# Contrast adjustment: every store on ScalarE's DMA queue, the last tile in two column halves, and sums shared with VectorE in all tiles

## The chip, the cores and the metric

The kernel runs on one core of one Trainium2 chip. The metric is device time in microseconds for one execution. Before the change it is 240.2 us, the median of 3 runs (240.01 to 240.23). One more execution was profiled; all views below are of that one.

## The reference

```
mean = np.mean(x, axis=(2, 3), keepdims=True)
return np.clip(mean + factor * (x - mean), 0, 1).astype(np.float32)
```

`x` is float32 of shape 16 x 3 x 512 x 512, 50.33 MB, and the output has the same size; `factor` is 1.5. Each of the 48 images of 512 x 512 has its own mean, and a pixel can be finished only when its whole image has been summed.

## The kernel before, in words

The input is read as 6 tiles of 128 partitions x 16384 floats (64 KB in a partition, 8.39 MB in a tile). A tile holds 8 images of 16 partitions each. Three tiles fit in SBUF: `ring` has `BUFS = 3` slots, and tile t lies in slot t mod 3. So the load of tile t+3 waits until every store of tile t has landed. Everything is done in place in the slot.

The steps of one tile are:

- **Load** (`load`, L78): a DMA issued by SyncE (SP). Tile 0 comes in three pieces (2048, 6144 and 8192 columns), the others whole.
- **Sum** (`add`, `sum_up`, L87 and L90): ScalarE (ACT) copies a range of columns onto itself with `accum_out`, which leaves each partition's sum. VectorE (DVE) sums another range with a `tensor_reduce`. For tile 0 each half is shared (VectorE takes `SUM` = 4352 columns and ScalarE 3840 of each half). For tiles 1 and 2 VectorE takes 4352 and ScalarE 12032 columns. For tiles 3, 4 and 5 ScalarE sums all 16384 columns.
- **Shift** (L104): TensorE multiplies the partial sums by `blockw`, a block matrix with `(1 - factor) / n_pix` in blocks of 16 x 16. This adds the 16 partitions of each image and leaves the shift of every partition in PSUM. There is one matmul in the code for each partial sum, accumulated.
- **Clip** (L107 and L110): two VectorE `tensor_scalar` instructions over a range of columns, x * factor + shift, then max 0 and min 1. Both lines together are called the clip pair below.
- **Store** (`store`, L81): a DMA issued by the queue that is handed in. The stores of tiles 0, 1 and 2 and the first quarter of tile 3 (4096 columns) are issued by ScalarE; the other three quarters of tile 3, and tiles 4 and 5 whole, by SP.

The order on each engine is the order in the code, since the schedule is written out by hand. Each engine takes its instructions strictly in order, DMA issues included: an issue that waits for a semaphore holds up whatever stands behind it on its engine. SP issues all 8 loads first (the loads of tiles 3, 4 and 5 each with their waits), and then the three last stores. ScalarE alternates sums and stores until the first quarter of tile 3, and has only sums after that.

In the text, "store 3a" is the first quarter of tile 3 and "store 3b" its other three quarters. A "row" of a DMA is what it moves for one partition: 128 rows in each DMA, 64 KB long for a whole tile, and shorter for a range of columns.

Of the kernel before, what the change touches and what calls it, by code (L numbers as in the profile page):

```python
# [1 line left out]

# [4 lines left out]


P = 128  # L10
ROW = 16384
HALF = ROW // 2
BUFS = 3
SHORT = 2048
SUM = 4352
QUARTER = ROW // 4


@with_exitstack
def kernel(  # L20
    ctx: ExitStack,
    tc: tile.TileContext,
    x: bass.AP,
    factor: float,
    out: bass.AP,
):

    nc = tc.nc  # L30
    f32 = mybir.dt.float32
    Alu = mybir.AluOpType
    Act = mybir.ActivationFunctionType

    B, C, H, W = x.shape
    n_img, n_pix = B * C, H * W
    ppi = n_pix // ROW
    per_tile = P // ppi
    n_tiles = n_img // per_tile
    assert ppi * ROW == n_pix and per_tile * n_tiles == n_img  # L40

    factor = float(factor)
    wconst = (1.0 - factor) / float(n_pix)

    x_f = x.rearrange("b c h w -> (b c h w)")
    out_f = out.rearrange("b c h w -> (b c h w)")

    def dram(ap, t, c0=0, c1=ROW):
        return bass.AP(tensor=ap.tensor, offset=t * P * ROW + c0, ap=[[ROW, P], [1, c1 - c0]])

    consts = ctx.enter_context(tc.tile_pool(name="consts", bufs=1))
    xpool = ctx.enter_context(tc.tile_pool(name="xpool", bufs=1))
    small = ctx.enter_context(tc.tile_pool(name="small", bufs=1))
    psum = ctx.enter_context(tc.tile_pool(name="psum", bufs=1, space=bass.MemoryType.PSUM))


    sums = small.tile([P, 4 * n_tiles], f32, name="sums")
    bias = psum.tile([P, n_tiles], f32, name="bias")

    blockw = consts.tile([P, P], f32, name="blockw")  # L60
    blocks = blockw.rearrange("p (a b) -> p a b", b=ppi)
    nc.gpsimd.memset(blockw, wconst)  # L62
    for base, step in ((0, -ppi), (ppi - 1, ppi)):
        nc.gpsimd.affine_select(  # L64
            out=blocks,
            in_=blocks,
            compare_op=Alu.is_ge,
            fill=0.0,
            base=base,
            pattern=[[step, per_tile], [0, ppi]],  # L70
            channel_multiplier=1 if step < 0 else -1,
        )


    ring = xpool.tile([P, BUFS, ROW], f32, name="ring")

    def load(t, c0=0, c1=ROW):
        return nc.sync.dma_start(out=ring[:, t % BUFS, c0:c1], in_=dram(x_f, t, c0, c1))  # L78

    def store(queue, t, c0=0, c1=ROW):  # L80
        queue.dma_start(out=dram(out_f, t, c0, c1), in_=ring[:, t % BUFS, c0:c1])  # L81

    def add(t, col, c0, c1, c2):
        xt = ring[:, t % BUFS, :]
        own = sums[:, 4 * t + col : 4 * t + col + 2]
        part = xt[:, c1:c2]
        nc.scalar.activation(out=part, in_=part, func=Act.Copy, accum_out=own[:, 0:1])  # L87
        if c0 == c1:
            return [own[:, 0:1]]
        nc.vector.tensor_reduce(  # L90
            out=own[:, 1:2], in_=xt[:, c0:c1], axis=mybir.AxisListType.X, op=Alu.add
        )
        return [own[:, 0:1], own[:, 1:2]]

    def sum_up(t):
        if t == 0:
            return add(t, 0, 0, SUM, HALF) + add(t, 2, HALF, HALF + SUM, ROW)
        return add(t, 0, 0, SUM if t < BUFS else 0, ROW)

    def clip(t, parts, *cuts):  # L100
        xt = ring[:, t % BUFS, :]
        shift = bias[:, t : t + 1]
        for k, part in enumerate(parts):
            nc.tensor.matmul(shift, blockw, part, start=k == 0, stop=k == len(parts) - 1)  # L104
        for c0, c1 in zip((0, *cuts), (*cuts, ROW)):
            part = xt[:, c0:c1]
            nc.vector.tensor_scalar(  # L107
                out=part, in0=part, scalar1=factor, scalar2=shift, op0=Alu.mult, op1=Alu.add
            )
            nc.vector.tensor_scalar(  # L110
                out=part, in0=part, scalar1=0.0, scalar2=1.0, op0=Alu.max, op1=Alu.min
            )

    with tc.manual_schedule():
        load(0, 0, SHORT)
        load(0, SHORT, HALF)
        load(0, HALF, ROW)
        load(1)
        load(2)
        clip(0, sum_up(0), SHORT, HALF)  # L120
        store(nc.scalar, 0, 0, SHORT)
        store(nc.scalar, 0, SHORT, HALF)
        store(nc.scalar, 0, HALF, ROW)
        for t in range(1, BUFS):
            clip(t, sum_up(t))
            store(nc.scalar, t)
        for t in range(BUFS, n_tiles):
            load(t)
        clip(BUFS, sum_up(BUFS), QUARTER)
        store(nc.scalar, BUFS, 0, QUARTER)  # L130
        store(nc.sync, BUFS, QUARTER, ROW)
        for t in range(BUFS + 1, n_tiles):
            clip(t, sum_up(t))
            store(nc.sync, t)


# [1 line left out]
_INS = ['x', 'factor']  # L138
_OUTS = [((16, 3, 512, 512), 'float32')]

_NUMBERS = {'factor': 1.5}


# [26 lines left out]
```

## Time and profile before

| what | value |
|---|---|
| time, median of 3 runs | 240.2 us (240.01 to 240.23) |
| the profiled execution's own time | 239.29 us |
| its span in the profile | 237.5 us |
| VectorE busy | 124.2 us (52% of the span) |
| ScalarE busy | 70.8 us (30%) |
| TensorE busy | 6.1 us (3%) |
| bytes moved | 50.33 MB read, 50.33 MB written |

The span runs from the first to the last instruction or DMA of the program that the profile holds; the 1.8 us by which the execution's own time is longer lie around it. The page's DMA row gives the mean busy share of the core's 16 DMA engines in 40 equal slices of 5.94 us, in tenths; the row under it gives the GB/s of each slice. A DMA row's bytes are put down to the slice in which it starts, so single slices can show more than the DMA engines can move, with less beside them. Section 3 of the page lists the DMA queues: q1 is SP's and q10 ScalarE's. Section 4 is the chain of work that ended last, followed back from the end.

### The profile page before, as it was taken

How to read it: one execution, taken by the hardware profiler on the slowest of the kernel's cores; microseconds unless marked ns; L12 is line 12 of the kernel's file. 1: busy time of each engine (PE TensorE's matmuls, PEld its weight loads, DVE VectorE, ACT ScalarE, POOL GpSimd, SP SyncE). 2: the span in 40 equal slices, each digit the busy share in tenths (PEclk: the TensorE clock that was granted, in tenths of full speed). 3: DMA queues.
4: the chain of work that ended last, by engine and by line, in shares of the span. 5: the costliest groups of instructions: out<-in, count | busy, mean ns of one | idle time of the engine just before them, and what ended most of it. 6: DMA issues, size and time to landing. Idle time of an engine off the chain costs nothing.

```text
span 237.5 us, 176 instructions
## 1 busy us (share of the span) xinstructions
PE 6.1 (3%) x22; PEld 5.4 (2%) x22; DVE 124.2 (52%) x22; ACT 70.8 (30%) x15; POOL 1.1 (0%) x7
## 2 busy tenths in 40 slices
PE   0010100001000010000000000000000000000000
PEld 0010100001000010000000000000000000000000
DVE  0071899952999429960000049950059936992000
ACT  2051300195001950000009940009931992000000
POOL 1000000000000000000000000000000000000000
DMA  7999989999999998989898998989997999999894
GB/s 292 414 441 441 530 360 397 419 399 429 444 410 425 425 530 353 530 353 530 353 497 386 441 441 386 497 345 439 428 544 345 488 414 475 408 408 475 353 530 177
DMA packets 2448, 100.66 MB, mean 424 GB/s; under 512 B 272, under 2 KB 272, under 8 KB 272
## 3 DMA queue, kind: packets, MB, share of 16 engines
q1 hardware_dynamic: 1584, 73.40, 72.0%
q10 hardware_dynamic: 864, 27.26, 26.6%
HBM read 50.33 MB, written 50.33 MB: 424 GB/s over the span
## 4 chain that ended last, share of the span: by engine, by line
DMA 38%; DVE 24%; another core or an unknown queue 16%; ACT 10%; PE 1%; SPq 1%; issue 0%; ACTq 0%; DVEq 0%
DMA ring<-in_x_dram 20%; DMA out_dram<-ring 18%; DVE ring L107 11%; DVE ring L110 11%; ACT ring L87 10%; DVE sums L90 2%; PE bias L104 1%; SPq L78 1%; ACTq L81 0%; ACTq L165 0%; DVEq L107 0%
## 5 line engine op out<-in xcount | busy, mean ns | idle before, releaser
L87 ACT ACTIVATE ring<-ring 128x16384 f32<-128x16384 f32 (+2 forms) x7 | 68.8, 9833 | 125.8 <-DMA ring<-in_x_dram 86.2
L107 DVE TENSOR_SCALAR ring<-ring,bias 128x16384 f32<-128x16384 f32 (+5 forms) x9 | 53.2, 5911 | 73.2 <-PE bias L104 73.2
L110 DVE TENSOR_SCALAR ring<-ring 128x16384 f32<-128x16384 f32 (+5 forms) x9 | 52.6, 5849 | 0.3
L90 DVE TENSOR_REDUCE sums<-ring 128x1 f32<-128x4352 f32 x4 | 18.7, 4683 | 17.9 <-DMA ring<-in_x_dram 17.9
L104 PE MATMUL bias<-sums,blockw 128*128 128x1 f32 x22 | 6.1, 359 | 191.9 <-ACT ring L87 190.7
L104 PEld LDWEIGHTS bias<-sums,blockw 128*128 128x128 f32 x22 | 5.4, 316 | 192.6 <-ACT ring L87 174.7
L87 ACT ACT_TABLE_LOAD x1 | 1.3, 1283 | 0.8 <-PEq L151 0.8
L87 ACT ACTIVATION_READ_ACCUMULATOR ring<-ring 128x1 f32 x7 | 1.3, 186 | 0.0
L64 POOL TENSOR_SCALAR_AFFINE_SELECT blockw<-blockw 128x128 f32<-128x128 f32 x2 | 0.7, 340 | 0.1
L62 POOL MEMSET blockw<- 128x128 f32 x1 | 0.2, 204 | 0.3 <-POOLq L151 0.3
L151 POOL MEMSET const-bfloat16-1.0<- 128x1 bf16 x1 | 0.1, 101 | 0.0
L151 POOL MEMSET const-uint8-127<- 128x1 uint8 x1 | 0.1, 101 | 0.0
L151 POOL MEMSET const-float32-0.0<- 128x1 f32 x1 | 0.1, 98 | 0.3 <-issue 0.3
L151 POOL MEMSET const-float32-1.0<- 128x1 f32 x1 | 0.1, 98 | 0.0
## 6 DMA issues: line engine op xcount, KB each, us to landing
out_dram<-ring SPq DMA_DIRECT2D x1, 6144.0 KB, 40.3
ring<-in_x_dram SPq DMA_DIRECT2D x1, 4096.0 KB, 20.9
out_dram<-ring ACTq DMA_DIRECT2D x1, 4096.0 KB, 35.6
ring<-in_x_dram SPq DMA_DIRECT2D x1, 3072.0 KB, 11.6
out_dram<-ring ACTq DMA_DIRECT2D x1, 3072.0 KB, 34.7
out_dram<-ring ACTq DMA_DIRECT2D x1, 2048.0 KB, 34.1
ring<-in_x_dram SPq DMA_DIRECT2D x1, 1024.0 KB, 4.8
out_dram<-ring ACTq DMA_DIRECT2D x1, 1024.0 KB, 26.4
```

What stands on the lines that cost most here:

```text
L62: nc.gpsimd.memset(blockw, wconst)
L64: nc.gpsimd.affine_select(out=blocks, in_=blocks, compare_op=Alu.is_ge, fill=0.0, base=base, pattern=[[step, per_tile], [0, ppi]], channel ...
L78: return nc.sync.dma_start(out=ring[:, t % BUFS, c0:c1], in_=dram(x_f, t, c0, c1))
L87: nc.scalar.activation(out=part, in_=part, func=Act.Copy, accum_out=own[:, 0:1])
L90: nc.vector.tensor_reduce(out=own[:, 1:2], in_=xt[:, c0:c1], axis=mybir.AxisListType.X, op=Alu.add)
L104: nc.tensor.matmul(shift, blockw, part, start=k == 0, stop=k == len(parts) - 1)
L107: nc.vector.tensor_scalar(out=part, in0=part, scalar1=factor, scalar2=shift, op0=Alu.mult, op1=Alu.add)
L110: nc.vector.tensor_scalar(out=part, in0=part, scalar1=0.0, scalar2=1.0, op0=Alu.max, op1=Alu.min)
L151: nc = _bacc.Bacc("TRN2", target_bir_lowering=False, num_devices=1)
```

## The change

- All stores are issued by ScalarE. SP has loads alone.
- VectorE sums `WIDE` = 7424 columns of tiles 1, 2, 3 and 4, and ScalarE the other 8960. Of tile 5, ScalarE sums the first half (8192 columns) alone; of the second half VectorE sums 4352 and ScalarE 3840 columns.
- Tile 5 is loaded, clipped and stored in two halves of 8192 columns each.
- Loads are written beside the tile that runs two tiles earlier, instead of ahead of all; on SP, which has nothing else left, their order is the same as before.

The core of the diff:

```diff
+WIDE = 7424
-    def store(queue, t, c0=0, c1=ROW):
-        queue.dma_start(out=dram(out_f, t, c0, c1), in_=ring[:, t % BUFS, c0:c1])
+    def store(t, c0=0, c1=ROW):
+        nc.scalar.dma_start(out=dram(out_f, t, c0, c1), in_=ring[:, t % BUFS, c0:c1])
...
-        return add(t, 0, 0, SUM if t < BUFS else 0, ROW)
...
+    first = ((0, SHORT), (SHORT, HALF), (HALF, ROW))
+    whole = ((0, ROW),)
+    middle = ((0, QUARTER), (QUARTER, ROW))
+    last = ((0, HALF), (HALF, ROW))
+    end = n_tiles - 1
...
-        for t in range(BUFS, n_tiles):
-            load(t)
-        clip(BUFS, sum_up(BUFS), QUARTER)
-        store(nc.scalar, BUFS, 0, QUARTER)
-        store(nc.sync, BUFS, QUARTER, ROW)
-        for t in range(BUFS + 1, n_tiles):
-            clip(t, sum_up(t))
-            store(nc.sync, t)
+        for t in range(1, end):
+            if t + 2 <= end:
+                for c0, c1 in last if t + 2 == end else whole:
+                    load(t + 2, c0, c1)
+            shift_by(t, add(t, 0, 0, WIDE, ROW))
+            for c0, c1 in middle if t == BUFS else whole:
+                clip(t, c0, c1)
+                store(t, c0, c1)
+        shift_by(end, add(end, 0, 0, 0, HALF) + add(end, 2, HALF, HALF + SUM, ROW))
+        for c0, c1 in last:
+            clip(end, c0, c1)
+            store(end, c0, c1)
```

In the changed kernel the matmuls (`shift_by`) and the clip pair (`clip`, now for one range of columns) are two functions. What they compute is the same.

More of the change, by code (lines that the diff above doesn't have):

```diff
@@ L77, in load @@
     def load(t, c0=0, c1=ROW):
-        return nc.sync.dma_start(out=ring[:, t % BUFS, c0:c1], in_=dram(x_f, t, c0, c1))
-    def store(queue, t, c0=0, c1=ROW):
-        queue.dma_start(out=dram(out_f, t, c0, c1), in_=ring[:, t % BUFS, c0:c1])
+        nc.sync.dma_start(out=ring[:, t % BUFS, c0:c1], in_=dram(x_f, t, c0, c1))
+    def store(t, c0=0, c1=ROW):
+        nc.scalar.dma_start(out=dram(out_f, t, c0, c1), in_=ring[:, t % BUFS, c0:c1])
     def add(t, col, c0, c1, c2):
@@ L93, in add @@
         return [own[:, 0:1], own[:, 1:2]]
-    def sum_up(t):
-        if t == 0:
-            return add(t, 0, 0, SUM, HALF) + add(t, 2, HALF, HALF + SUM, ROW)
-        return add(t, 0, 0, SUM if t < BUFS else 0, ROW)
-    def clip(t, parts, *cuts):
-        xt = ring[:, t % BUFS, :]
-        shift = bias[:, t : t + 1]
-        for k, part in enumerate(parts):
[L104 to L108, printed above, removed]
-            )
-            nc.vector.tensor_scalar(
-                out=part, in0=part, scalar1=0.0, scalar2=1.0, op0=Alu.max, op1=Alu.min
-            )
@@ L114, with shift_by @@
-    with tc.manual_schedule():
[L115 to L123, printed above, removed]
+    def shift_by(t, parts):
+        for k, part in enumerate(parts):
+            nc.tensor.matmul(
+                bias[:, t : t + 1], blockw, part, start=k == 0, stop=k == len(parts) - 1
+            )
@@ new lines, in clip @@
+    def clip(t, c0=0, c1=ROW):
+        part = ring[:, t % BUFS, c0:c1]
+        nc.vector.tensor_scalar(
+            out=part, in0=part, scalar1=factor, scalar2=bias[:, t : t + 1],
+            op0=Alu.mult, op1=Alu.add,
+        )
+        nc.vector.tensor_scalar(
+            out=part, in0=part, scalar1=0.0, scalar2=1.0, op0=Alu.max, op1=Alu.min
+        )
+    first = ((0, SHORT), (SHORT, HALF), (HALF, ROW))
+    whole = ((0, ROW),)
+    middle = ((0, QUARTER), (QUARTER, ROW))
+    last = ((0, HALF), (HALF, ROW))
@@ L124 @@
+    end = n_tiles - 1
+    with tc.manual_schedule():
+        for c0, c1 in first:
+            load(0, c0, c1)
         for t in range(1, BUFS):
-            clip(t, sum_up(t))
-            store(nc.scalar, t)
-        for t in range(BUFS, n_tiles):
             load(t)
-        clip(BUFS, sum_up(BUFS), QUARTER)
-        store(nc.scalar, BUFS, 0, QUARTER)
-        store(nc.sync, BUFS, QUARTER, ROW)
-        for t in range(BUFS + 1, n_tiles):
-            clip(t, sum_up(t))
-            store(nc.sync, t)
+        shift_by(0, add(0, 0, 0, SUM, HALF) + add(0, 2, HALF, HALF + SUM, ROW))
+        for c0, c1 in first:
+            clip(0, c0, c1)
+            store(0, c0, c1)
+        for t in range(1, end):
[10 more added lines that the diff above has]
+            store(end, c0, c1)
```

## The prediction

> **What bounds the kernel now.** I read the page's slices first, then its queues, and only then the chain of waits.
>
> ```profile
> DVE  0071899952999429960000049950059936992000
> ACT  2051300195001950000009940009931992000000
> ...
> DMA  7999989999999998989898998989997999999894
> GB/s 292 414 441 441 530 360 397 419 399 429 444 410 425 425 530 353 530 353 530 353 497 386 441 441 386 497 345 439 428 544 345 488 414 475 408 408 475 353 530 177
> DMA packets 2448, 100.66 MB, mean 424 GB/s; under 512 B 272, under 2 KB 272, under 8 KB 272
> ...
> q1 hardware_dynamic: 1584, 73.40, 72.0%
> q10 hardware_dynamic: 864, 27.26, 26.6%
> ```
>
> VectorE and ScalarE have slices of 0; the DMA row has none. The queues add up to 72.0 + 26.6 = 98.6% of what 16 engines could have been busy, 234.2 of 237.5 us. The rest lies at the two ends: SP's first issue is at 0.80 us and the first bytes move at 1.8, and about 1.3 us pass between the last row's end (236.3) and the end of the span. The chain of waits gives 24% to VectorE and 10% to ScalarE, but it follows one dependence: beside each of those pieces the DMA engines were moving another tile. Stretches of the windows view, cut at events, show it:
>
> ```profile
> 1.80:22.60 20.80, 1.14 (x4) 1.00 (x4) 4.69 (x2) 3.77 (x4) 0.02 (x1) 1.00 1.07 453
> 75.70:118.40 42.70, 1.02 (x4) 0.93 (x4) 21.91 (x3) 10.32 (x2) 0.00 (x0) 1.00 1.02 442
> 183.40:215.60 32.20, 0.59 (x2) 0.50 (x2) 26.39 (x4) 13.95 (x2) 0.00 (x0) 1.00 1.00 431
> ```
>
> The last two columns are DMA share and GB/s: loads alone, loads beside stores, and stores alone all fill the engines (shares over 1 come from booking a row where it starts). So **the bytes bound the span**. Making data ready earlier gains only where the DMA engines would have had nothing to move, and loses only where it leaves them so.
>
> **How two queues share.** Packets: 17 DMAs x 128 rows + 17 x 16 semaphore writes = 2448, so a packet is one partition's row, 8 rows on each of 16 engines for each DMA. Section 6 of the page has a 1024 KB store that took 26.4 us to land beside whole-tile loads. Sharing by bytes would need 2 MB, 5 us; one 8 KB row in turn with one 64 KB row needs 8 x 72 KB x 16 = 9.4 MB, 22 us at 424 GB/s. So queues take turns row by row, and short rows get little. The trace's packet records give a row's time on its engine: 2.42 us for 64 KB, 1.815 for 48 KB, 1.213 for 32 KB, 0.61 for 16 KB.
>
> **The end before.** Load 5 lands at 183.4, its last row at 182.6. Then only stores are left, in one queue: store 3b takes 8 x 1.815 = 14.5, store 4 takes 8 x 2.42 = 19.3, drained at 216.4 (the records: 216.05). Tile 5 meanwhile:
>
> ```profile
> 183.44 13.86 ACT L87 ACTIVATE ring<-ring 128x16384 f32<-128x16384 f32 x1 [9.23 <-DMA ring<-in_x_dram]
> ...
> 198.07 8.76 DVE L107 TENSOR_SCALAR ring<-ring,bias 128x16384 f32<-128x16384 f32 x1 [5.69 <-PE bias L104]
> 206.86 8.70 DVE L110 TENSOR_SCALAR ring<-ring 128x16384 f32<-128x16384 f32 x1
> ```
>
> Its store is issued at 215.6 and needs 1.0 us until bytes move (0.80 to 1.8 at the start). It lands in 21.0 us, the shortest of line L81, which is 1.0 + 19.3 and a landing of 0.8: it waited behind nothing. So there is a **hole of about 0.2 us** here (216.05 to 216.4 in the records, 0.16 as a mean over engines). It is the only hole between start and end.
>
> **The change part by part.**
>
> *Sums shared.* A VectorE sum of 4352 took 4.68, so 7424 takes up to 8.0; ScalarE's 8960 take 10.23 x 8960/12032 = 7.6. A tile is summed in 8.0 instead of 10.2 or 13.9. Clips start about 2.4 us earlier for tile 1, 5 for tile 2 (both gains in sequence) and 5.5 for tiles 3 and 4. VectorE gains 2 x 3.3 + 2 x 8.0 + 4.7 = 27 us of work on 124, in its slices of 0. Stores 1 to 4 are issued earlier and wait longer in a queue that already has work: worth 0, and the cover is the full DMA row. Four more matmuls (8 rows of 0.36 us) sit in the same idle time.
>
> *Stores on ScalarE.* Three more issues of 0.34 us. What stands behind them on ScalarE: behind store 3b the sum of tile 4, whose load lands only at 160.3, while that store is issued at about 152; behind store 4, the sum of tile 5, costed below. SP loses three issues behind which nothing stood. What does move is the turn-taking: before, store 3b (157.6) stood behind load 5 (156.9) in SP's queue; now it takes turns with load 5.
>
> *The last tile in halves, step by step.* Load 5 is issued at 156.9 as before, since it waits for store 2, whose bytes nothing ahead of it changes. From about 159.5 (load 4's last row) store 3a has some 7 rows left, in turn with load 5's first half: 7 x (0.61 + 1.213) = 12.8, to 172.3. Then store 3b in turn with the remaining 9 load rows: 8 x (1.815 + 1.213) + 1.2 = 25.4, to 197.7. The second half lands at 198.5, **15 us later than load 5 did**. Store 4, alone then, is drained at 197.7 + 19.3 = 217.0. Tile 4: landed 160.3, summed 168.3, clip from 169.5, store 4 issued at 187.0. The first half's sum waits on ScalarE until 187.0 and takes 13.86/2 = 6.9, to 194: early enough, this is its cover. The second half: VectorE's 4.7 to 203.2, matmuls about 1, a clip pair over 8192 of 4.48 + 4.43 (rows of tile 0) to 213.1. First store issued then, bytes from 214.1, against 217.0: **2.9 us to spare**. Second store at 222.0, bytes from 223.0, against 217.0 + 9.7 = 226.7: 3.7 to spare. The hole goes: -0.2. Next comes nothing; the queue is full to the end.
>
> *Shorter rows.* Two more DMAs: two rows of 32 KB take 2 x 1.213 against 2.418, 0.008 us more; 8 pairs on each engine, load and store: +0.13.
>
> In this trace tile 0's three loads, 8.39 MB, landed at 22.6: 1.8 + 19.3 of rows + 0.8 of landing = 21.9, so two boundaries and a slow first row cost at most 0.7 us together. A rule of the Trainium skill speaks against the halves: "SBUF — State Buffer", section "The DMA setup-cost knee", puts a roughly fixed 2 us on every DMA. By that the two extra DMAs would cost 4 us and the kernel would take 244; the row says that the fixed part lies under the next DMA's rows.
>
> **Sum**: 237.5 - 0.2 + 0.13 = 237.4 for the span. The profiled execution's own time is 239.29, so 239.2 for its like; the median of the runs, 240.2, lies 0.9 above it with no part of the trace to tell why, so I carry the difference over: **240.1**. A measurement of this kernel can tell about 0.2% (0.48 us) from no change.
>
> **Unknown costs, from both sides.** 32 KB load rows in turn with 48 KB store rows do not occur before. Below: the records show rows slowed by 1.07 us in all (0.55 between 30 and 42 us, 0.53 between 53 and 60, in both just as a piece of store 0 begins beside a load); were all of it a matter of turns that happen to fall better, the gain is 1.1. Above: the slowest 64 KB load row took 2.96 against 2.42, 22%; if all 16 rows of load 5 did that, 16 x 1.213 x 0.22 = +4.3. The nearest row, store 3a beginning beside loads 4 and 5, shows nothing, so I take 0.
>
> **Rivals.**
>
> 1. *The new turns slow rows* (slower). Place: 172 to 198, where store 3b begins beside load 5. Price: each such beginning cost 0.5 with store 0, so 240.6 to 241.1 for one or two. For: two of the three beginnings of a short-rowed store beside a load were slow. Against: store 3a was not. It decides from one beginning on.
> 2. *Load 5 comes too late* (slower). Taking turns puts it at 198.5 with 2.9 us to spare; every us beyond costs one. If the queues gave stores two rows a turn, store 4 too would be gone before load 5 is in, and sum, matmuls and half a clip, 4.7 + 1 + 8.9 = 15 us, would lie bare: up to 255. Against: the 26.4 us row says one by one.
> 3. *More goes than the hole* (faster). The 0.9 us by which the runs exceed the profiled execution may be a wider hole at 216, as its two sides differ by only 0.4; or the slowed rows vanish. 239.1 to 239.7.
> 4. *The sums as gain*. By the chain, tile 5's path is 13.9 - 6 and half a clip shorter: some 15 us. Against: 98.6%. I give it nothing.
>
> **How the numbers follow.** Forecast 0.60 (239.8 to 240.6), rival 1 0.19, rival 2 0.04, rival 3 0.17. Faster 0.17, within 0.2% 0.60, slower 0.23. The range leaves out rival 2, the ends of rivals 1 and 3 and the 4.3: 239.2 to 241.2.
>
> **What would show it.** In the changed profile: queue shares still summing to about 98.6%, now with equal bytes; no slice of DMA below 8 between the first and the last; the second half of load 5 landing near 198, not 183; store 4 issued near 187, tile 5's stores near 213 and 222, both landing later than an empty queue would allow (over 11.5 us). A span off by more than 0.5 with full shares means rows slowed (rival 1, or less of it: rival 3); a hole around 217 means rival 2. The forecast is wrong if rows' times depend on what they alternate with.

## The result and the profile after

The changed kernel takes **248.5 us** (median of 6 runs, 245.2 to 251.1) against 240.2 (239.2 to 240.8): the ratio is 1.031, with a 95% interval from 1.025 to 1.038. The forecast was 240.1, and the range ended at 241.2. The ratio leaves out the two longest of the six runs (250.9 and 251.1), which count as a slower state; by the medians as they stand it would be 1.035. The profiled execution took 245.24 and is the shortest of the six; its span is 243.5 us, 6.0 longer than before. All readings of the changed kernel's trace below are of that execution.

The page of the changed kernel, the lines that answer to those of before:

```profile
DVE  0073899989999799300048999058997000899800
ACT  2053200390009300000048000056001900500000
...
DMA  7999889989899997979798999899999999846996
GB/s 301 463 436 511 355 355 409 575 384 389 370 447 431 431 517 345 517 345 517 345 517 355 506 398 463 366 425 441 431 436 425 447 474 431 388 215 258 431 431 258
DMA packets 2736, 100.66 MB, mean 413 GB/s; under 512 B 304, under 2 KB 304, under 8 KB 304
...
q1 hardware_dynamic: 1296, 50.33, 48.6%
q10 hardware_dynamic: 1440, 50.33, 47.9%
```

The DMA row now has an 8, a 4 and a 6 in slices 35 to 37, and GB/s falls to 215 and 258 there. The queues' shares add up to 96.5% of 243.5 = 235.0 us, against 234.2 before. So the rows took 0.8 us longer, and more than 5 us are a hole. The windows view of the changed kernel finds it (each line: the stretch and its length, the busy time of TensorE, its weight load, VectorE, ScalarE and GpSimd with the number of instructions, the granted clock, the DMA share and GB/s):

```profile
207.10:216.00 8.90, 1.17 (x4) 1.00 (x4) 8.13 (x2) 3.50 (x2) 0.00 (x0) 1.00 0.92 398
216.00:222.40 6.40, 0.00 (x0) 0.00 (x0) 6.37 (x3) 0.00 (x0) 0.00 (x0) 1.00 0.08 36
222.40:242.00 19.60, 0.00 (x0) 0.00 (x0) 7.94 (x2) 0.00 (x0) 0.00 (x0) 1.00 0.99 423
```

From 216 to 222.4 VectorE is clipping and the DMA engines have next to nothing to move. The chain of waits says what VectorE had been waiting for (start, duration, what; SPq is the sequencer of SyncE, which issues DMAs):

```profile
157.06 0.33 SPq L79
...
157.44 49.68 DMA ring<-in_x_dram
...
207.14 4.70 DVE sums L91
```

Load 5 is issued at 157, as before, but its second half lands at **207.1**. The forecast had 198.5; before, the whole of load 5 had landed at 183.4. What follows is as costed, in the timeline (start, duration, engine, line, operation; in brackets how long the engine was idle before it, and what ended that; ACTq lines are DMA issues by ScalarE):

```profile
187.37 0.34 ACTq L82 DMA_DIRECT2D out_dram<-ring  x1
187.81 7.03 ACT L88 ACTIVATE ring<-ring 128x8192 f32<-128x8192 f32 x1 [19.19 <-DVE ring L108]
...
207.14 4.69 DVE L91 TENSOR_REDUCE sums<-ring 128x1 f32<-128x4352 f32 x1 [19.86 <-DMA ring<-in_x_dram]
...
212.56 4.49 DVE L104 TENSOR_SCALAR ring<-ring,bias 128x8192 f32<-128x8192 f32 x1 [0.74 <-PE bias L98]
217.09 4.43 DVE L108 TENSOR_SCALAR ring<-ring 128x8192 f32<-128x8192 f32 x1
...
221.54 9.26 ACTq L82 DMA_DIRECT2D out_dram<-ring  x2
```

Store 4 is issued at 187.4 (forecast 187.0). The sum, matmuls and half a clip from the landing to the first store take 221.5 - 207.1 = 14.4 us (forecast 14.6). But most DMA engines are through with store 4 at 216 to 217 (the last at 219.4), and the first store of tile 5 has bytes to move only at 222.4.

### The profile page after: what moved, and what is told of

Its sections match the earlier page's. It is cut to its first block, busy times and chain, and to the rows that moved or that the text cites. A ratio compares the mean times of both kernels' runs of the same rounds, so it can differ in the third digit from the quotient of the medians.

```text
span 243.5 us, 205 instructions
## 1 busy us (share of the span) xinstructions
PE 8.1 (3%) x30; PEld 7.2 (3%) x30; DVE 151.3 (62%) x27; ACT 49.9 (21%) x17; POOL 1.1 (0%) x7
## 2 busy tenths in 40 slices
DMA packets 2736, 100.66 MB, mean 413 GB/s; under 512 B 304, under 2 KB 304, under 8 KB 304
## 4 chain that ended last, share of the span: by engine, by line
DMA 47%; DVE 26%; another core or an unknown queue 16%; ACT 3%; PE 1%; SPq 1%; issue 0%; ACTq 0%; DVEq 0%
DMA ring<-in_x_dram 29%; DMA out_dram<-ring 19%; DVE ring L104 11%; DVE ring L108 11%; DVE sums L91 4%; ACT ring L88 3%; PE bias L98 1%; SPq L79 1%; ACTq L82 0%; DVEq L104 0%
## 5 line engine op out<-in xcount | busy, mean ns | idle before, releaser
L91 DVE TENSOR_REDUCE sums<-ring 128x1 f32<-128x7424 f32 (+1 forms) x7 | 45.6, 6513 | 72.0 <-DMA ring<-in_x_dram 72.0
L88 ACT ACTIVATE ring<-ring 128x8960 f32<-128x8960 f32 (+2 forms) x8 | 47.9, 5990 | 159.9 <-DMA ring<-in_x_dram 101.1
L104 DVE TENSOR_SCALAR ring<-ring,bias 128x8192 f32<-128x8192 f32 (+5 forms) x10 | 53.4, 5342 | 6.7 <-PE bias L98 6.7
L108 DVE TENSOR_SCALAR ring<-ring 128x8192 f32<-128x8192 f32 (+5 forms) x10 | 52.8, 5280 | 0.3
L98 PE MATMUL bias<-sums,blockw 128*128 128x1 f32 x30 | 8.1, 359 | 204.3 <-ACT ring L88 202.5
L98 PEld LDWEIGHTS bias<-sums,blockw 128*128 128x128 f32 x30 | 7.2, 317 | 205.2 <-ACT ring L88 186.7
```

Of the source, the lines that this page charges most:

```text
L91: nc.vector.tensor_reduce(out=own[:, 1:2], in_=xt[:, c0:c1], axis=mybir.AxisListType.X, op=Alu.add)
L98: nc.tensor.matmul(bias[:, t : t + 1], blockw, part, start=k == 0, stop=k == len(parts) - 1)
L104: nc.vector.tensor_scalar(out=part, in0=part, scalar1=factor, scalar2=bias[:, t : t + 1], op0=Alu.mult, op1=Alu.add,)
L108: nc.vector.tensor_scalar(out=part, in0=part, scalar1=0.0, scalar2=1.0, op0=Alu.max, op1=Alu.min)
```

## The experiments

**Theory T (turns).** Load 5 and the stores lie in different queues and take turns row by row, whatever a row's length. Load rows half as long need twice as many turns, and are passed by twice as many store rows. Load 5's landing then sets the end. **Rivals:** A, the split tail costs in itself (two more DMAs, short rows), or ScalarE's order does; S, the shared sums do, because store 4 comes earlier.

In the short diffs the base is the changed kernel ("after") or the kernel before, as named.

### Load 5 whole, all else of the change kept (after)

```diff
-                for c0, c1 in last if t + 2 == end else whole:
+                for c0, c1 in whole:
                     load(t + 2, c0, c1)
```

> The changed kernel with one edit: tile 5 is loaded whole (64 KB rows), its clip and its stores stay in halves. Theory T (turns): queues take turns row by row, so load 5 with 8 long rows per DMA engine is passed by only 8 store rows (4 left of store 3a, 4 of store 3b) instead of 16; it starts at 160.8 and lands near 160.8 + 4 x 3.03 + 4 x 4.23 + 0.8 = 190.6, not 207; tile 5's first store is issued near 211 while store 4 is drained near 216.5, so there is no hole: 239.5 to 240.5 us. Theory A (two stores and a split tail cost in themselves, or ScalarE's order does): the hole at 216 to 222 stays and the time stays near 246 to 250. Theory S (shared sums are to blame, since store 4 comes earlier): stays near 246 to 250.

Measured: 240.25 us, ratio 0.999 (0.997 to 1.001). In the timeline VectorE's sum of tile 5, which waits for load 5, and the two stores of tile 5; in the windows view the stretch where the hole was:

```profile
194.14 4.68 DVE L91 TENSOR_REDUCE sums<-ring 128x1 f32<-128x4352 f32 x1 [6.55 <-DMA ring<-in_x_dram]
...
214.81 9.24 ACTq L82 DMA_DIRECT2D out_dram<-ring  x2
```
```profile
216.00:222.00 6.00, 0.00 (x0) 0.00 (x0) 5.97 (x2) 0.00 (x0) 0.00 (x0) 1.00 0.99 426
```

Load 5 landed at 194.1, not 207.1 (T had 190.6), and the DMA engines are full. The same bytes in the same queues: only the rows are twice as long, in one DMA instead of two. The split clip and stores, the shared sums and ScalarE's queue stayed, so A and S fall as causes of the loss.

### Store 3b on SP, behind load 5 (after)

```diff
-    def store(t, c0=0, c1=ROW):
-        nc.scalar.dma_start(...)
+    def store(t, c0=0, c1=ROW, queue=nc.scalar):
+        queue.dma_start(...)
...
-                store(t, c0, c1)
+                store(t, c0, c1, nc.sync if t == BUFS and c0 else nc.scalar)
```

> The changed kernel with one edit: store 3b (three quarters of tile 3) is issued by SP, behind both halves of load 5 in the same queue; all other stores stay on ScalarE. Theory T: load 5's 16 rows pass 4 rows of store 3a and then go alone: 160.8 + 4 x 1.82 + 12 x 1.213 + 0.8 = 183.5 landing; no hole; 239.5 to 240.5 us. Theories A and S: unchanged from the changed kernel, 246 to 250.

Measured: 240.41 us, ratio 1.001 (0.999 to 1.003). In its packet records load 5's last row ends at 184.5, and store 3b's first row starts only at 182.3, on an engine that is through with load 5. The hole is gone:

```profile
216.00:222.00 6.00, 0.00 (x0) 0.00 (x0) 1.72 (x1) 0.00 (x0) 0.00 (x0) 1.00 1.00 431
```

One store of 6.29 MB in the other queue takes the whole loss away.

### The halves alone, and the sums alone (before)

```diff
+        load(n_tiles - 1, 0, HALF)
+        load(n_tiles - 1, HALF, ROW)
...
+        clip(t, add(t, 0, 0, 0, HALF) + add(t, 2, HALF, HALF + SUM, ROW), HALF)
+        store(nc.sync, t, 0, HALF)
+        store(nc.sync, t, HALF, ROW)
```

> The kernel before with the halves alone: tile 5 loaded, summed (first half by ScalarE, second shared), clipped and stored in two halves, every store on the queue it had before. Theory T: the stores 3b and 4 stand behind load 5 in SP's queue, so short rows harm nothing; load 5 lands near 183.5, the first half's store is issued near 207, before store 4 is drained at 216: hole gone, 239.7 to 240.3 us. Theory A: 245 or more.

Measured: 240.18 us, ratio 1.001 (0.999 to 1.003).

```diff
-        return add(t, 0, 0, SUM if t < BUFS else 0, ROW)
+        return add(t, 0, 0, WIDE, ROW)
```

> The kernel before with the shared sums alone (VectorE 7424 columns of tiles 1 to 5, ScalarE 8960), all queues and tile 5 whole as before. Theory T: harmless: store 4 and store 5 are issued earlier and the hole of 0.2 us goes: 239.7 to 240.3 us. Theory S: 243 or more.

Measured: 239.23 us, ratio 0.999 (0.997 to 1.001). Neither part costs anything where the stores 3b and 4 stand behind load 5, and a gain of 0.2 us from the hole before is too small for these intervals.

### Everything but the queues (before)

The two edits above together, the sums of tiles 1 to 4 with `WIDE`, and every store in the queue of before.

> Everything of the change but the queues: the shared sums and the last tile in halves, with the stores 3b, 4 and 5 on SP as in the kernel before. Theory T: load 5 lands near 183 as before, the stores of tile 5 wait in a full queue; no hole, 239.5 to 240.2 us. If the loss needed no queue: 245 or more.

Measured: 240.6 us, ratio 1.001 (1.000 to 1.003): no loss without the queue change, nor a gain.

### The queues alone (before)

```diff
-        store(nc.sync, BUFS, QUARTER, ROW)
+        store(nc.scalar, BUFS, QUARTER, ROW)
...
-            store(nc.sync, t)
+            store(nc.scalar, t)
```

> The kernel before with the queues alone: every store on ScalarE, tile 5 whole, sums as before. Theory T: load 5 (64 KB rows) lands near 190.6, later than 183.4, but that is not what decides here: ScalarE's 13.9 us sum of tile 5 now stands behind store 4's issue at 192.4, so it ends near 206.7, the clip pair ends near 225, bytes move from 226 while store 4 is drained near 216.3: a hole of about 10 us, 249 to 251 us. If sharing of a queue by itself made loads as late as in the changed kernel (207 or later), it would be 255 to 260. Theory A: no halves, so 240.

Measured: 249.1 us, ratio 1.038 (1.034 to 1.041). The timeline of ScalarE:

```profile
192.92 0.34 ACTq L81 DMA_DIRECT2D out_dram<-ring  x1
193.70 13.86 ACT L87 ACTIVATE ring<-ring 128x16384 f32<-128x16384 f32 x1 [18.97 <-DMA ring<-in_x_dram]
...
225.84 0.34 ACTq L81 DMA_DIRECT2D out_dram<-ring  x1
```

The queue change alone loses as much as the whole change, though partly by another way. Load 5, whole, lands at 193.7, some 10 us later than before, and only then can the sum of 13.9 us start (store 4's issue, from 192.9 to 193.3, would have held it up almost as long). Turn-taking is there too; the shared sums and halves would hide this much of it, as the run with load 5 whole shows.

### The sums of before in the changed kernel (after)

```diff
-            shift_by(t, add(t, 0, 0, WIDE, ROW))
+            shift_by(t, add(t, 0, 0, SUM if t < BUFS else 0, ROW))
```

> The changed kernel with one edit: the sums of tiles 1 to 4 are split as in the kernel before (VectorE 4352 columns of tiles 1 and 2, none of 3 and 4). Theory T: store 4 is issued near 193 instead of 187, store 3b is drained before its first row, and about one and a half rows of load 5 go alone; load 5 lands near 204, 3 us earlier: hole near 3.5, 243 to 247 us, a little faster than the changed kernel. Theory S (the shared sums' early stores are the cause): the whole loss goes, 240. Rival: VectorE's shares are needed, and without them it is slower, 250 or more.

Measured: 243.08 us, ratio 1.015 (1.010 to 1.020), faster than the changed kernel, as T asked. VectorE's sum of the second half:

```profile
204.54 4.68 DVE L91 TENSOR_REDUCE sums<-ring 128x1 f32<-128x4352 f32 x1 [11.64 <-DMA ring<-in_x_dram]
```

The landing is 2.6 us earlier, and so is the end of the span (240.9); by the medians the difference is 5.4. Store 4 is issued at 192.9 here, against 187.4. S is right in so far as the early store 4 makes it worse: its long rows get into the turns. It is not the cause by itself, since the sums without the queues cost nothing.

### Store 3 in other row lengths (after)

Whole (64 KB rows), in eight pieces (8 KB rows) and in four (16 KB rows):

```diff
-            for c0, c1 in middle if t == BUFS else whole:
+            for c0, c1 in whole:
```
```diff
-    middle = ((0, QUARTER), (QUARTER, ROW))
+    middle = tuple((c, c + SHORT) for c in range(0, ROW, SHORT))
```
```diff
-    middle = ((0, QUARTER), (QUARTER, ROW))
+    middle = tuple((c, c + QUARTER) for c in range(0, ROW, QUARTER))
```

> The changed kernel with one edit: tile 3 is clipped and stored whole (one store with 64 KB rows instead of 16 KB and 48 KB rows), so that load 5's 16 short rows meet only long store rows. Theory T: some 6.5 rows of store 3 and then rows of store 4 take turns with load 5: 6.5 x 3.63 + about 3 load rows alone until store 4 arrives at 188.4 + 6 x 3.63: load 5 lands near 212, tile 5's first bytes move near 227.5 against a queue drained near 215.5: a hole near 12 us, 250 to 256 us, slower than the changed kernel. Theories A and S: as the changed kernel, 246 to 250.

Measured: 248.0 us, ratio 1.033 (1.027 to 1.038), the same as the changed kernel. T had asked for 250 to 256, so this forecast is a miss, and the time tells nothing for T. The profiled execution, 253.1, is the longest of the five (the others took 246.5 to 249.8); in it load 5 landed later than in the changed kernel's:

```profile
215.08 4.69 DVE L91 TENSOR_REDUCE sums<-ring 128x1 f32<-128x4352 f32 x1 [24.92 <-DMA ring<-in_x_dram]
```

T had about 212. Since only this longest execution has a trace, I do not count it for T.

> The changed kernel with one edit in the other direction: tile 3 is clipped and stored in eight pieces of 2048 columns (8 KB rows, 64 rows per DMA engine). The bytes and their queue are the same; only the row length of the store that load 5 meets changes. Theory T: 16 turns of 1.213 + 0.31 = 24.4 us, load 5 lands near 186; no hole; eight times more rows cost some 0.5 us and the short rows may slow load rows by 0.5: 240 to 241.5 us. Theories A and S: 246 to 250 or more.

Measured: 246.1 us, ratio 1.026 (1.022 to 1.030). The number is a miss. The packet records have load 5's last row end at 184.4, as T asked, but ScalarE stood still:

```profile
136.55 37.27 ACTq L82 DMA_DIRECT2D out_dram<-ring  x8
173.87 7.67 ACT L88 ACTIVATE ring<-ring 128x8960 f32<-128x8960 f32 x1 [41.00 <-DMA ring<-in_x_dram]
```

The eight issues take 37 us, to 173.8, though the clips end at 153.8. In the trace the fourth to the eighth issue each wait first for the semaphore that they will use themselves and that an earlier DMA has used: the fifth comes at 160.6, when load 4 has landed at 160.5, and the seventh at 173.0, when load 5's first half has landed at 172.9. The sum of tile 4 stands behind them and begins 13 us late. That is a hole of another kind; the next run takes it away:

> The changed kernel with one edit: tile 3 is clipped and stored in four pieces of 4096 columns (16 KB rows, 32 per DMA engine) instead of one of 4096 and one of 12288. In the run with eight pieces load 5 had moved by 184, as theory T asked, but ScalarE was held up in its store issues, whose semaphores were in use; four pieces need no such wait. Theory T: 16 turns of 1.213 + 0.61 = 29 us, load 5 lands near 190, tile 4's sum starts at 161 as in the changed kernel, no hole: 239.5 to 240.7 us. Theory A (the halves cost in themselves): 246 to 250.

Measured: 240.65 us, ratio 1.001 (0.999 to 1.003). The timeline has VectorE's sum of the second half at:

```profile
191.68 4.69 DVE L91 TENSOR_REDUCE sums<-ring 128x1 f32<-128x4352 f32 x1 [4.34 <-DMA ring<-in_x_dram]
```

T had about 190. Load 5 is still in halves, all stores are still on ScalarE's queue, and store 3 has the same bytes. Shorter *store* rows alone bring the landing from 207.1 to 191.7 and the loss to nothing.

### Load 5 in four quarters (after)

```diff
-                for c0, c1 in last if t + 2 == end else whole:
+                for c0, c1 in fine if t + 2 == end else whole:
+    fine = tuple((c, c + QUARTER) for c in range(0, ROW, QUARTER))
```

> The changed kernel with one edit: load 5 in four quarters (16 KB rows, 32 per DMA engine) instead of two halves; clip and stores stay in halves. Theory T: twice as many turns. From 160.8 on, some 4 rows beside store 3a, 8 beside store 3b, a few alone until store 4 arrives at 188, 8 beside store 4 and the rest alone: load 5 lands near 217, after store 4 is drained. In the profiles of the changed kernel, of the one with the sums undone and of the one with store 3 whole, the span was load 5's landing plus 36.4 us (207.1 and 243.5, 204.5 and 240.9, 215.1 and 251.4), so 253 for the span, 252 to 257 for the time. Rival: the turns go by bytes, not rows; then the quarters change nothing, 246 to 250.

Measured: 258.2 us, ratio 1.073 (1.070 to 1.077).

```profile
220.38 4.69 DVE L91 TENSOR_REDUCE sums<-ring 128x1 f32<-128x4352 f32 x1 [32.95 <-DMA ring<-in_x_dram]
```

T had 217 for the landing and 253 for the span; they are 220.4 and 256.6, and the time is a little above T's range (252 to 257). Load rows of 64, 32 and 16 KB land load 5 at 194, 207 and 220. Turns by bytes would land all three alike, so that rival falls.

### What sets the end

Wherever the landing of load 5 is late, the span follows it at a fixed distance (profiled executions):

| kernel | load 5 landed | span | difference |
|---|---|---|---|
| sums of before | 204.5 | 240.9 | 36.4 |
| changed kernel | 207.1 | 243.5 | 36.4 |
| store 3 whole | 215.1 | 251.4 | 36.3 |
| load 5 in quarters | 220.4 | 256.6 | 36.2 |

The 36.4 are 14.4 from the landing to the first store's issue, about 1 until bytes move, 19.6 for both stores' rows (222.4 to 242.0) and 1.4 to the end.

### A version that might beat both (before, with the shared sums)

```diff
-        clip(0, sum_up(0), SHORT, HALF)
-        store(nc.scalar, 0, 0, SHORT)
-        store(nc.scalar, 0, SHORT, HALF)
-        store(nc.scalar, 0, HALF, ROW)
+        clip(0, sum_up(0))
+        store(nc.scalar, 0)
```

> The kernel before with shared sums (as in the run that had them alone) and with tile 0 clipped and stored whole. It asks whether the 1.07 us of slowed load rows of the kernel before come from the short rows of store 0's pieces beside loads. If so they vanish and the bytes end some 1 us earlier: 238.5 to 239.3 us, under 0.997 of the kernel before. If they come from something else: 239.3 to 240.2. A rival on the other side: tile 0's store begins 16 us later and load 3 with it: slower, if a hole opens.

Measured: 240.0 us, ratio 0.9995 (0.997 to 1.002): no gain. The packet records still have 1.15 us of slowed load rows, now between 42 and 53 us. So they do not come from the short rows of store 0's pieces; what they come from stays open. No version that I ran is faster than the kernel before beyond its interval.

## Why the prediction was wrong, point by point

- **What bounds the kernel** held: the bytes, with 234 to 235 us of DMA work in both profiles, and a hole as the only other price.
- **Sums shared**: sums of 7.7 and 7.9 us, store 4 at 187.4, 27 us more VectorE work (151.3 against 124.2): right. "Worth 0" was right without the queue change. Beside it, the early store 4 cost 2.6 us by the traces and 5.4 by the medians, which the prediction had not connected.
- **Stores on ScalarE** and **shorter rows**: nothing was lost by three more issues; the halves alone cost nothing that can be measured. The 4 us by the rule on fixed DMA costs did not come (240.2 with the halves alone).
- **The step that failed** is "the last tile in halves, step by step", in its first sentence on the turns: "From about 159.5 (load 4's last row) store 3a has some 7 rows left, in turn with load 5's first half". The packet records show load 5's first row at 160.8, and 4.5 of the 8 rows of store 3a already begun: 2.3 of them before 159.5, not one, and the others while SP's queue had no row to offer. So 3.5 short turns were left, not 7, and more of load 5 met long rows. I had taken one start time from an assumption, that a load's rows begin where the load ahead of it ends; the kernel before already had load 5's first row at 160.4, behind a last row of load 4 that ended at 159.2. I did not look.
- **What stood there instead**: the forecast's sum has no row of store 4 ahead of load 5's landing, and the records have 3.0 (all these are means over the 16 engines), 7.2 us. Two passed between load rows. The third passed between load 5's last row and its completion write, the 4-byte packet that reports the landing: this write moved 2.4 us after the last row, where the forecast let it follow at once, as it did in the kernel before. Against the forecast's sum the late start adds 1.6 us (161.1 against 159.5), the missing short rows take off 2.1, store 4's rows add 7.2, and slowed rows and small gaps some 1.9: 8.6 in all, from 198.5 to 207.1. The 2.9 us to spare were gone, and a hole of between 5 and 6 us remained. Even with 7 short turns the sum was a turn or two short: it has store 4 issued at 187.0 and load 5 ending near 197, so the last load row and the completion write would have met store 4's rows. That is 2.4 to 4.8 us, an estimate from the rows of 2.42, against 2.9 to spare.
- **Rival 2** was the right mechanism ("load 5 comes too late", every us beyond costs one), at a chance of 0.04, and its sign, "a hole around 217", is what the profile shows. I tied it to two rows a turn, which the 1024 KB store spoke against. It needed only fewer short rows left to meet, because each one that passes early saves 0.6 us and can put a row of 2.4 us ahead of the landing. A margin of 2.9 us with that leverage was no margin.
- **Rival 1** had little part: rows beside each other were slowed by 0.6 us between 150 and 215 (0.01 before).
- **What is open.** The account above is of the shortest execution, 245.24; the median is 3.3 us longer. The runs of the changed kernel spread from 245.2 to 251.1, those of the kernel before from 239.2 to 240.8. One row of store 3a more or less ahead of load 5 is worth 2.4 us, which would give such a spread, but the other executions have no trace; this was argued and not shown.

## What to carry to other kernels

Where DMA bounds the kernel, a load on which the end depends should not share the DMA engines with a backlog of long-rowed stores in another queue: in these runs queues took turns row by row, so the load's share was its row length against theirs, and cutting it into column pieces made it later. Put the stores that can wait behind it in its own queue, or keep its rows long. When a forecast rests on a margin, ask what one row of error does to it, take every start from the records, and count the completion write as a turn.

## What the runs showed of the hardware that I had not expected

- Queues that share the 16 DMA engines take turns by rows: rows of 64, 32 and 16 KB in the load against the same stores landed it at 194, 207 and 220, and store rows of 16 KB instead of 48 KB brought the 207 to 192. The Trainium skill, "DMA: Bandwidth & Descriptors", section "Queues, rings and completion order", says that a DMA engine goes round the queues that have work and drains a whole packet of one before the next. The trace agrees, with one row as a packet (2736 packets for 19 DMAs of 128 rows and 16 completion writes).
- The completion write took a turn too. Load 5's moved right behind its last row where no other queue had rows (the kernel before), but 0.6 us later beside 16 KB rows (store 3 in four), 1.7 beside 48 KB rows (load 5 whole) and 2.4 beside 64 KB rows (the changed kernel).
- Which engine issues a DMA is not only a matter of issue time. One store moved from ScalarE to SP took the time from 248.5 to 240.4. The same page, section "Issuing engines are not separate DMA queues", says that issuing from several engines only saves the sequencer's time; for bandwidth this trace agrees (431 to 433 GB/s either way), but the order in which transfers finish changed: load 5's last row ended at 184.5 with that store on SP and at 204.3 with it on ScalarE. Here the measurement decides.
- A load issued while the DMA engines were busy moved its first row 3.7 us after its issue (157.1 to 160.8; the load ahead of it in its queue had its last rows end at 158.0 to 159.9), against 1.0 at the start of the program.
- A store issue can hold up ScalarE by its semaphore: eight stores in a row stood for 37 us, and a sum behind them began 13 us late (173.9 against 160.9).
